# Where weights and features start within 512 bytes: a lead, a slot size and a gap in a float32r decoder trunk

## The chip, the core and the metric

The kernel runs on one core of a Trainium2 chip. The core has TensorE (PE in the profile; its weight loads are shown apart as PEld), VectorE (DVE), ScalarE (ACT), GpSimd (POOL) and SyncE (SP), which here issues nearly all transfers. They share SBUF, 128 partitions of on-chip memory, and TensorE writes its sums to PSUM. A matmul has a stationary operand, which is loaded into the array by a weight load, and a moving operand, which is streamed past it. The metric is the device time of one execution in microseconds (us), as the median of several runs.

## The reference, cut to what matters

Two decoder layers on 256 tokens of width 1024, in float32. Each layer adds four blocks to the residual x:

```python
for l in range(DEPTH):                       # 2 layers
    x = x + 0.5 * swiglu(rms_norm(x, ffn1_norm[l]), gate1[l], up1[l], down1[l])     # 1024 -> 2816 -> 1024
    x = x + hybrid_mixer(rms_norm(x, mix_norm[l]), w_in[l], ..., w_out[l])          # 4 scan heads, 8 softmax heads
    x = x + memory_cross_attention(rms_norm(x, cross_norm[l]), rms_norm(mem, mem_norm[l]),
                                   wq[l], wk[l], wv[l], wo[l])                      # 256 memory tokens
    x = x + 0.5 * swiglu(rms_norm(x, ffn2_norm[l]), gate2[l], up2[l], down2[l])
return rms_norm(x, final_norm)

def swiglu(h, w_gate, w_up, w_down):
    return (silu(h @ w_gate) * (h @ w_up)) @ w_down
```

Nearly all of the work is products of 256 token rows with weight matrices.

## The kernel before

**Precision by splitting.** A float32 product is made of three float32r matmuls. An operand `a` is split into `hi`, its value cast to float32r, and `lo = a - hi`. `mm3` (L441 to L444) then sums `hi*hi`, `hi*lo` and `lo*hi` in PSUM, so each product shows up as one matmul of L442, one of L443 and one of L444. Features are split once per block (`put_split`, L368); weights are split as they come in.

**The plan of weights.** `plan` lists all weight pieces in the order in which they are used: `add_cols` (L90) lists the pieces of a range of columns, four row tiles of 128 each; `add_rows` (L94) those of whole rows of 1024 columns, two row tiles each; `add_ffn` (L98) calls both. `fetch` (L129) loads a piece from HBM into one of three `raw` buffers, by a transfer on SP. `split` (L173) casts it on ScalarE into a `whi` slot and subtracts on VectorE into a `wlo` slot (`split_k`, L145 to L155; L149 and L150 without a gain, L153 and L154 with one). There are seven slots of each kind (`N_W`), of SLOT = 1040 columns. A slot takes two row tiles of 512 columns, one of 1024, or four of 260. `take` (L194) hands out the next piece and has the piece after it split (`LA_S` = 1); the loads run three pieces ahead (`LA_D`). The first two pieces are split block by block in `split_block` (L157).

**Two ways round.** In `wstat` (L566) the weights are stationary and the features move: 256 columns, all tokens, move past a block of 128x128 weights, and the result has features on the partitions. This serves the gate and up projections from the second chunk of columns on, the mixer's gates, queries and keys, and the queries and keys of the cross attention. In `xstat`, `xstat_first`, `first_chunk` and `rows_to_residual` (L450, L460, L482, L637) a block of features is stationary and the weights move, 512 columns at a time (256 or 260 for some): the first chunk of each gate and up projection, the values, the down projections and the output projections. In `rows_to_residual`, while it walks over the row tiles, a slot of one row tile serves twelve matmuls before the next one.

**Memory.** Each pool's tiles lie one behind another in SBUF, in the order of the pools: constants (`cp`), `raw`, the `whi` slots and then the `wlo` slots (`wp`), 19 buffers of 4096 bytes with the tag `s4` (`sp`), which hold the features and nearly all intermediate tiles, then `np` and `sm` with smaller ones, among them `pp` and `ppT`, tiles of the softmax. Below them lie 16384 bytes of scratch for transfer descriptors. Sizes here are bytes per partition.

**Order.** `drive` (L403) runs the main generator and spawned tasks by modelled times, so that small tasks (norms, transposes, softmax heads) are put between the large products in TensorE's instruction stream. In the cross attention, `head` (L1113) uses `mm3` too, without weights: `cs` is the score of a query tile `qc` (stationary) with `kc` (moving), and `cpo` the value tile `vch` or `vcl` (stationary) with the transposed probabilities `ppT` (moving). All of them but `ppT` carry the tag `s4`.

Of the kernel before, what the change touches and what calls it, by code (L numbers as in the profile page):

```python
# [8 lines left out]
F32 = mybir.dt.float32  # L9
# [8 lines left out]
P = 128  # L18
DEPTH = 2
S = 256  # L20
D = 1024
# [4 lines left out]
EPS = 1e-6  # L26
NEG = -1.0e30
FCH = [(c, min(512, DFF - c)) for c in range(0, DFF, 512)]
SLOT = 1040
N_S4, N_W = 19, 7  # L30
TAIL = 6
HP = 100
# [8 lines left out]
OFF_Q, OFF_F, OFF_I, OFF_G = 0, 512, 1024, 1536  # L41
OFF_FQ, OFF_FK, OFF_FV = 2048, 2560, 3072
# [3 lines left out]
def hymba_kernel(  # L46
# [6 lines left out]
    nc = tc.nc  # L53

    cp = ctx.enter_context(tc.tile_pool(name="cp", bufs=1))
    rawp = ctx.enter_context(tc.tile_pool(name="rawp", bufs=3))
    wp = ctx.enter_context(tc.tile_pool(name="wp", bufs=N_W))
    sp = ctx.enter_context(tc.tile_pool(name="sp", bufs=N_S4))
# [7 lines left out]
    def nm(s):  # L66
        uid[0] += 1
        return f"{s}_{uid[0]}"
# [10 lines left out]
    def smp(name="smp"):  # L79
        return pss.tile([P, 512], F32, name=nm(name), tag="smp")  # L80

    xs = cp.tile([P, NT, D], F32, name="xs")


    plan = []

    def kview(w, l, c0, cw, k0, nk):
        return w[l, k0 * P:(k0 + nk) * P, c0:c0 + cw].rearrange("(k p) c -> p k c", p=P)

    def add_cols(w, l, c0, cw, scaled=None):  # L90
        for k0 in range(0, KT, 4):
            plan.append((kview(w, l, c0, cw, k0, 4), 4, cw, (scaled[0], scaled[1] + k0) if scaled else None))

    def add_rows(w, l, nkt):  # L94
        for k0 in range(0, nkt, 2):
            plan.append((kview(w, l, 0, D, k0, 2), 2, D, None))

    def add_ffn(g, u, d, l, scaled=None):  # L98
        for c0, cw in FCH:
            add_cols(g, l, c0, cw, scaled)  # L100
            add_cols(u, l, c0, cw, scaled)
        add_rows(d, l, FT)

    for l in range(DEPTH):
        add_ffn(ffn1_g, ffn1_u, ffn1_d, l, ("first", 0) if l == 0 else None)
        for o in (OFF_I, OFF_G, OFF_F, OFF_Q):
            add_cols(w_in, l, o, 512)
        add_cols(w_in, l, OFF_FV + 260, 260)
        add_cols(w_in, l, OFF_FQ, 512)
        add_cols(w_in, l, OFF_FK, 512)  # L110
        add_cols(w_in, l, OFF_FV, 260)
        of_mem = ("mem", 8 * l)
        add_cols(c_wk, l, 0, 512, of_mem)
        add_cols(c_wk, l, 512, 512, of_mem)
        add_cols(c_wv, l, 0, 512, of_mem)
        add_rows(w_out, l, KT)
        add_cols(c_wv, l, 512, 512, of_mem)
        for c0 in (0, 512):
            add_cols(c_wq, l, c0, 512)
        add_rows(c_wo, l, KT)  # L120
        add_ffn(ffn2_g, ffn2_u, ffn2_d, l)

    raws = []
# [4 lines left out]

    def fetch(i):  # L129
        while len(raws) <= min(i, len(plan) - 1):  # L130
            src, nk, cw, _ = plan[len(raws)]
            r = rawp.tile([P, 4 * 520], F32, name=nm("raw"), tag="raw")
            rv = r[:, :nk * cw].rearrange("p (k c) -> p k c", k=nk)
            n = 4 if len(raws) < 2 else 1
            for k0 in range(0, nk, nk // n):
                nc.sync.dma_start(out=rv[:, k0:k0 + nk // n, :], in_=src[:, k0:k0 + nk // n, :])
                for t, j in ({0: [(1, 0)], 3: [(0, 1), (1, 1)]}.get(k0, []) if not raws else []):
                    load_x(t, j)
            raws.append(r)

    def load_x(t, j):
        sl = slice(j * 512, (j + 1) * 512)
        nc.sync.dma_start(out=xs[:, t, sl], in_=x_d[0, t * P:(t + 1) * P, sl])

    def split_k(i, sl, k, hi, lo):  # L145

        gk = plan[i][3]
        if gk is None:
            nc.scalar.copy(out=hi, in_=sl)  # L149
            nc.vector.tensor_tensor(out=lo, in0=sl, in1=hi.bitcast(F32), op=ALU.subtract)  # L150
        else:
            g = gcols[gk[0]][:, gk[1] + k:gk[1] + k + 1]
            nc.scalar.mul(hi, sl, g)  # L153
            nc.vector.scalar_tensor_tensor(out=lo, in0=sl, scalar=g, in1=hi.bitcast(F32), op0=ALU.mult,  # L154
                                           op1=ALU.subtract)  # L155

    def split_block(i, k):  # L157

        if k == 0:
            fetch(i + LA_D - 1)  # L160
            pieces.append([])
        cw = plan[i][2]
        if k % 2 == 0:
            slot[:] = [wp.tile([P, SLOT], F32R, name=nm(n), tag=n) for n in ("whi", "wlo")]
        sl = slice(k % 2 * cw, (k % 2 + 1) * cw)
        hi, lo = slot[0][:, sl], slot[1][:, sl]
        split_k(i, raws[i][:, k * cw:(k + 1) * cw], k, hi, lo)
        pieces[i].append((hi, lo))
        return [(hi, lo)]
# [3 lines left out]
    def split(i):  # L173
        while len(pieces) <= min(i, len(plan) - 1):
            j = len(pieces)
            fetch(j + LA_D - 1)
            _, nk, cw, gk = plan[j]
            r = raws[j]
            n = max(1, SLOT // cw)
            res = []  # L180
            for k0 in range(0, nk, n):
                kk = min(n, nk - k0)
                sl = r[:, k0 * cw:(k0 + kk) * cw]
                hi = wp.tile([P, SLOT], F32R, name=nm("whi"), tag="whi")
                lo = wp.tile([P, SLOT], F32R, name=nm("wlo"), tag="wlo")
                n1 = kk if gk is None else 1
                for k in range(0, kk, n1):
                    w = slice(k * cw, (k + n1) * cw)
                    split_k(j, sl[:, w], k0 + k, hi[:, w], lo[:, w])
                for k in range(kk):  # L190
                    res.append((hi[:, k * cw:(k + 1) * cw], lo[:, k * cw:(k + 1) * cw]))
            pieces.append(res)

    def take():  # L194
        i = taken[0]
        taken[0] += 1
        split(i + LA_S)
        return pieces[i]
# [18 lines left out]
    for i in range(2):  # L217
        fetch(i)
# [998 lines left out]
```

## Time and profile before

| | |
|---|---|
| median of 3 runs | 1233.07 us (1232.48 to 1235.84) |
| the profiled execution | 1233.42 us |
| its span, first to last instruction | 1231.3 us |
| mean granted TensorE clock | 0.999 |
| read from HBM, mean rate | 216.23 MB, 176 GB/s |

The profile shows one execution. Its page gives, in parts, the engines' busy time, the span in 40 slices, the DMA queues, the chain of work that ended last, the costliest groups of instructions, and the DMA issues. A group's row has the line of the code, engine, operation, what it writes and reads (`out<-in`; for a matmul the moving operand stands first and the stationary one second), shapes, the count, busy time, the mean duration of one, and the idle time just before. Matmuls overlap: one of 256 columns is shown as about 280 ns long, yet the next starts well before it has ended. The timeline has one row per instruction with its start and its duration in us; from two starts and the number of matmuls between them comes the step from one matmul to the next. Addresses aren't in the profile; they follow from the sizes in the code.

### The profile page before, as it was taken

What the parts mean: (1) busy time and instruction counts of PE and PEld (TensorE: products, weight loads), DVE (VectorE), ACT (ScalarE), POOL (GpSimd) and SP (SyncE); (2) the same over time, 40 slices, a digit from 0 to 9 for tenths busy, and PEclk for the clock granted to TensorE, in tenths of its full rate; (3) what the DMA queues carried; (4) which work ended last, traced back from release to release, by engine and by line L of the source; (5) the groups of instructions that cost most, each with busy time, mean ns of one, the idle gap of its engine ahead of it and who ended that gap; (6) DMA issues with size and microseconds to landing.
All of it is one profiled execution on the core that took longest, in us unless ns stands there. A gap on an engine that the chain in (4) does not pass through costs nothing.

```text
span 1231.3 us, 21555 instructions
## 1 busy us (share of the span) xinstructions
PE 1221.1 (99%) x9037; PEld 1117.8 (91%) x9037; DVE 769.6 (63%) x1186; ACT 650.4 (53%) x1014; POOL 37.1 (3%) x50
## 2 busy tenths in 40 slices
PE   9999999999999999999999999999999999999997
PEld 7999888999889889998889998889998898999986
DVE  6966647588866665554474464476787766545643
ACT  7655535578854454444354354266686555443532
POOL 0000000011000000000000000000110000000000
PEclk9999999999999999999999999999999999999999
DMA  8655655642544375565374565465444533555650
GB/s 296 203 177 175 240 196 159 218 159 104 204 141 152 115 244 172 172 223 189 134 256 139 204 201 209 137 222 168 144 138 171 189 137 122 196 179 171 240 171 35
DMA packets 100001, 218.67 MB, mean 178 GB/s; under 512 B 4128, under 2 KB 16704, under 8 KB 99904
## 3 DMA queue, kind: packets, MB, share of 16 engines
q1 hardware_dynamic: 99744, 217.03, 51.8%
q8 instruction: 71, 1.16, 0.4%
q10 hardware_dynamic: 160, 0.27, 0.1%
q14 instruction: 26, 0.21, 0.1%
HBM read 216.23 MB, written 1.05 MB: 176 GB/s over the span
## 4 chain that ended last, share of the span: by engine, by line
PE 93%; DVE 4%; issue 1%; ACT 1%; POOL 1%; DMA 0%; POOLq 0%; ACTq 0%
PE acc L442 28%; PE acc L443 28%; PE acc L444 28%; DVE wlo L150 1%; PE acc L505 1%; PE al L771 1%; DVE wlo L154 1%; PE pt L363 1%; POOL rs L344 1%; PE fs L933 0%; PE fpt L951 0%; DVE xfl L370 0%; PE cpo L443 0%; PE cs L444 0%; PE cs L442 0%
## 5 line engine op out<-in xcount | busy, mean ns | idle before, releaser
L150 DVE TENSOR_TENSOR wlo<-raw,whi 128x1024 fp32r<-128x1024 f32 (+1 forms) x324 | 388.9, 1223 | 265.5 <-ACT whi L149 264.6
L149 ACT CAST whi<-raw 128x1024 fp32r<-128x1024 f32 (+1 forms) x324 | 330.2, 1048 | 276.1 <-PE acc L444 132.5
L442 PE MATMUL acc<-xfh,whi 128*128 128x256 f32 x1536 | 432.2, 282 | 0.0
L443 PE MATMUL acc<-xfl,whi 128*128 128x256 f32 x1536 | 430.7, 280 | 0.3 <-DVE xfl L370 0.2
L444 PE MATMUL acc<-xfh,wlo 128*128 128x256 f32 x1536 | 429.9, 280 | 0.0
L443 PEld LDWEIGHTS acc<-xfl,whi 128*128 128x128 f32 x1536 | 289.3, 188 | 0.9 <-DVE xfl L370 0.7
L444 PEld LDWEIGHTS acc<-xfh,wlo 128*128 128x128 f32 x1536 | 289.3, 188 | 0.0
L442 PEld LDWEIGHTS acc<-xfh,whi 128*128 128x128 f32 x1536 | 288.5, 188 | 0.8
L443 PE MATMUL acc<-wlo,hth 128*128 128x512 f32 (+1 forms) x352 | 136.2, 387 | 0.0
L442 PE MATMUL acc<-whi,hth 128*128 128x512 f32 (+1 forms) x352 | 136.0, 386 | 0.0
L444 PE MATMUL acc<-whi,htl 128*128 128x512 f32 (+1 forms) x352 | 135.6, 385 | 0.0
L442 PE MATMUL acc<-whi,xfh 128*128 128x512 f32 (+1 forms) x240 | 88.0, 367 | 0.0
L443 PE MATMUL acc<-wlo,xfh 128*128 128x512 f32 (+1 forms) x240 | 87.4, 364 | 0.0
L444 PE MATMUL acc<-whi,xfl 128*128 128x512 f32 (+1 forms) x240 | 87.2, 363 | 0.0
L444 PEld LDWEIGHTS acc<-whi,htl 128*128 128x128 f32 x352 | 66.2, 188 | 14.2
L442 PEld LDWEIGHTS acc<-whi,hth 128*128 128x128 f32 x352 | 66.1, 188 | 14.1
L443 PEld LDWEIGHTS acc<-wlo,hth 128*128 128x128 f32 x352 | 66.1, 188 | 13.8
L154 DVE SCALAR_TENSOR_TENSOR wlo<-raw,g,whi 128x512 fp32r<-128x512 f32 (+1 forms) x96 | 62.0, 703 | 18.6 <-PE acc L444 14.9
L153 ACT ACTIVATE whi<-raw,g 128x512 fp32r<-128x512 f32 (+1 forms) x96 | 58.3, 677 | 17.2 <-PE acc L443 14.8
L369 ACT CAST hth<-sil 128x512 fp32r<-128x512 f32 x36 | 22.3, 619 | 57.4 <-DVE sil L738 57.4
L444 PEld LDWEIGHTS acc<-whi,xfl 128*128 128x128 f32 x240 | 45.2, 188 | 7.6
L442 PEld LDWEIGHTS acc<-whi,xfh 128*128 128x128 f32 x240 | 45.1, 188 | 7.7
(274 smaller groups left out, 1547.6 us busy)
## 6 DMA issues: line engine op xcount, KB each, us to landing
raw<-in_ffn_w_down_dram SPq DMA_DIRECT2D x44, 1024.0 KB, 4.9
raw<-in_ffn_w_up_dram SPq DMA_DIRECT2D x40, 1024.0 KB, 5.3
raw<-in_ffn_w_gate_dram SPq DMA_DIRECT2D x38, 1024.0 KB, 5.2
raw<-in_w_in_dram SPq DMA_DIRECT2D x24, 1024.0 KB, 5.3
raw<-in_cross_wk_dram SPq DMA_DIRECT2D x8, 1024.0 KB, 5.4
raw<-in_cross_wv_dram SPq DMA_DIRECT2D x8, 1024.0 KB, 5.2
raw<-in_w_out_dram SPq DMA_DIRECT2D x8, 1024.0 KB, 4.8
raw<-in_cross_wq_dram SPq DMA_DIRECT2D x8, 1024.0 KB, 5.2
```

The lines of the kernel that those rows point to most:

```text
L149: nc.scalar.copy(out=hi, in_=sl)
L150: nc.vector.tensor_tensor(out=lo, in0=sl, in1=hi.bitcast(F32), op=ALU.subtract)
L153: nc.scalar.mul(hi, sl, g)
L154: nc.vector.scalar_tensor_tensor(out=lo, in0=sl, scalar=g, in1=hi.bitcast(F32), op0=ALU.mult, op1=ALU.subtract)
L344: nc.gpsimd.tensor_tensor(out=rs, in0=ms, in1=neghalf[:, 0:1], op=ALU.pow)
L363: nc.tensor.transpose(pt[:, j * P:(j + 1) * P], hn[:, kt * P:(kt + 1) * P], ident)
L369: nc.scalar.copy(out=hi, in_=src)
L442: nc.tensor.matmul(ps, lhsT=lh, rhs=rh, start=start, stop=False)
L443: nc.tensor.matmul(ps, lhsT=lh, rhs=rl, start=False, stop=False)
L444: nc.tensor.matmul(ps, lhsT=ll, rhs=rh, start=False, stop=stop)
L505: nc.tensor.matmul(psa_[t], lhsT=x, rhs=w, start=kt == 0 and which == 0, stop=kt == KT - 1 and which == 1)
L771: nc.tensor.matmul(ps[s0:s0 + hb, c0:c0 + hb], lhsT=k[:, h, a:a + hb], rhs=rhs[:, h, a + step:a + step + hb], start=True, stop=True)
```

## The change

The slots become 1152 columns (4608 bytes), a multiple of 512 bytes. Row tiles within a slot start at multiples of 512 columns (256 for pieces of 256 columns), so that a 260-column row tile takes the room of 512 and a slot holds two of them. Each plan entry carries a lead: stationary weights start 16 columns (64 bytes) into their slot, moving ones at its start. A tile of 64 columns (256 bytes), `apart`, is put ahead of the `s4` buffers. To make room, the `raw` buffers lose 32 columns each and the scratch for transfer descriptors is halved to 8192 bytes. The products, their order and the loads stay.

```diff
-SLOT = 1040
+ROWS, LEAD = 1024, 16
+SLOT = ROWS + 128
+APART = 64
...
+    sp.tile([P, APART], F32, name="apart", tag="apart", bufs=1)
     xs = cp.tile([P, NT, D], F32, name="xs")
...
-    def add_cols(w, l, c0, cw, scaled=None):
+    def add_cols(w, l, c0, cw, scaled=None, lead=LEAD):
         for k0 in range(0, KT, 4):
-            plan.append((kview(w, l, c0, cw, k0, 4), 4, cw, (scaled[0], scaled[1] + k0) if scaled else None))
+            plan.append((kview(w, l, c0, cw, k0, 4), 4, cw, (scaled[0], scaled[1] + k0) if scaled else None, lead))
...
-            plan.append((kview(w, l, 0, D, k0, 2), 2, D, None))
+            plan.append((kview(w, l, 0, D, k0, 2), 2, D, None, 0))
...
-            add_cols(g, l, c0, cw, scaled)
-            add_cols(u, l, c0, cw, scaled)
+            for w in (g, u):
+                add_cols(w, l, c0, cw, scaled, LEAD if c0 else 0)
...
-            add_cols(w_in, l, o, 512)
-        add_cols(w_in, l, OFF_FV + 260, 260)
+            add_cols(w_in, l, o, 512, None, 0 if o in (OFF_I, OFF_G) else LEAD)
+        add_cols(w_in, l, OFF_FV + 260, 260, None, 0)
...
-            r = rawp.tile([P, 4 * 520], F32, name=nm("raw"), tag="raw")
+            r = rawp.tile([P, 4 * 512], F32, name=nm("raw"), tag="raw")
...
-            n = max(1, SLOT // cw)
+            step = 256 if cw == 256 else max(512, cw)
+            n = ROWS // step
...
+                hv, lv, rv = (a[:, b:b + kk * st].rearrange("p (k c) -> p k c", k=kk)[:, :, 0:cw]
+                              for a, b, st in ((hi, lead, step), (lo, lead, step), (sl, 0, cw)))
                 n1 = kk if gk is None else 1
                 for k in range(0, kk, n1):
-                    w = slice(k * cw, (k + n1) * cw)
-                    split_k(j, sl[:, w], k0 + k, hi[:, w], lo[:, w])
+                    w = slice(k, k + n1)
+                    split_k(j, rv[:, w], k0 + k, hv[:, w], lv[:, w])
                 for k in range(kk):
-                    res.append((hi[:, k * cw:(k + 1) * cw], lo[:, k * cw:(k + 1) * cw]))
+                    res.append((hv[:, k], lv[:, k]))
...
-    nc = _bacc.Bacc("TRN2", target_bir_lowering=False, num_devices=1)
+    nc = _bacc.Bacc("TRN2", target_bir_lowering=False, num_devices=1, dynamic_dma_scratch_size=8192)
```

The other 260-column piece and the values of the cross attention (`c_wv`) get a lead of 0 in the same way.

More of the change, by code (lines that the diff above doesn't have):

```diff
@@ L106, in hymba_kernel @@
         for o in (OFF_I, OFF_G, OFF_F, OFF_Q):
-            add_cols(w_in, l, o, 512)
-        add_cols(w_in, l, OFF_FV + 260, 260)
+            add_cols(w_in, l, o, 512, None, 0 if o in (OFF_I, OFF_G) else LEAD)
+        add_cols(w_in, l, OFF_FV + 260, 260, None, 0)
         add_cols(w_in, l, OFF_FQ, 512)
         add_cols(w_in, l, OFF_FK, 512)
-        add_cols(w_in, l, OFF_FV, 260)
+        add_cols(w_in, l, OFF_FV, 260, None, 0)
         of_mem = ("mem", 8 * l)
@@ L114, in hymba_kernel @@
         add_cols(c_wk, l, 512, 512, of_mem)
-        add_cols(c_wv, l, 0, 512, of_mem)
+        add_cols(c_wv, l, 0, 512, of_mem, 0)
         add_rows(w_out, l, KT)
-        add_cols(c_wv, l, 512, 512, of_mem)
+        add_cols(c_wv, l, 512, 512, of_mem, 0)
         for c0 in (0, 512):
@@ L130, in fetch @@
         while len(raws) <= min(i, len(plan) - 1):
-            src, nk, cw, _ = plan[len(raws)]
-            r = rawp.tile([P, 4 * 520], F32, name=nm("raw"), tag="raw")
+            src, nk, cw, _, _ = plan[len(raws)]
+            r = rawp.tile([P, 4 * 512], F32, name=nm("raw"), tag="raw")
             rv = r[:, :nk * cw].rearrange("p (k c) -> p k c", k=nk)
@@ L176, in split @@
             fetch(j + LA_D - 1)
-            _, nk, cw, gk = plan[j]
+            _, nk, cw, gk, lead = plan[j]
             r = raws[j]
-            n = max(1, SLOT // cw)
+            step = 256 if cw == 256 else max(512, cw)
+            n = ROWS // step
             res = []
```

## The prediction

> **What bounds the kernel now.** I read the page from the top: the engines' busy time, the granted clock, the chain that ended last, then the groups.
>
> ```profile
> span 1231.3 us, 21555 instructions
> ## 1 busy us (share of the span) xinstructions
> PE 1221.1 (99%) x9037; PEld 1117.8 (91%) x9037; DVE 769.6 (63%) x1186; ACT 650.4 (53%) x1014; POOL 37.1 (3%) x50
> ...
> PEclk9999999999999999999999999999999999999999
> ...
> PE 93%; DVE 4%; issue 1%; ACT 1%; POOL 1%; DMA 0%; POOLq 0%; ACTq 0%
> ...
> L150 DVE TENSOR_TENSOR wlo<-raw,whi 128x1024 fp32r<-128x1024 f32 (+1 forms) x324 | 388.9, 1223 | 265.5 <-ACT whi L149 264.6
> L149 ACT CAST whi<-raw 128x1024 fp32r<-128x1024 f32 (+1 forms) x324 | 330.2, 1048 | 276.1 <-PE acc L444 132.5
> ```
>
> The matmuls are the bound: PE is busy for 99% of the span at the full clock and makes 93% of the chain. The weight splits (cast on ACT, subtraction on DVE) wait for PE to give slots back, not the reverse. So the time is the number of matmuls times the step from one to the next. The mean of one (282 ns) is no step, as matmuls overlap; I take the step from the timeline, first start to last start of an unbroken stretch, and the count from the groups in the same stretch. Weights stationary (256 moving columns), in FFN 2 of the first layer:
>
> ```profile
> L442 PE MATMUL acc<-xfh,whi 128*128 128x256 f32 x279 | 78.2, 280 | 0.0
> L443 PE MATMUL acc<-xfl,whi 128*128 128x256 f32 x279 | 78.2, 280 | 0.0
> L444 PE MATMUL acc<-xfh,wlo 128*128 128x256 f32 x279 | 78.1, 280 | 0.0
> ```
> ```profile
> 457.02 0.36 PE L442 MATMUL acc<-xfh,whi 128*128 128x256 f32 x1
> ...
> 555.41 0.27 PE L444 MATMUL acc<-xfh,wlo 128*128 128x256 f32 x1
> ```
>
> 3·279 = 837 matmuls start in 98.39 us: 98.39/836 = **117.7 ns** a step. Weights moving (512 columns), the down projection of FFN 1:
>
> ```profile
> L442 PE MATMUL acc<-whi,hth 128*128 128x512 f32 x85 | 33.4, 392 | 0.0
> ```
> ```profile
> 135.14 0.39 PE L442 MATMUL acc<-whi,hth 128*128 128x512 f32 x1
> ...
> 193.84 0.39 PE L444 MATMUL acc<-whi,htl 128*128 128x512 f32 x1
> ```
>
> 3·85 = 255 matmuls in 58.70 us: 58.70/254 = **231.1 ns**. Nothing interrupts either stretch, so whatever varies in these steps is TensorE's own. The numbers of such matmuls in the kernel, by form:
>
> ```profile
> L442 PE MATMUL acc<-xfh,whi 128*128 128x256 f32 x1536 | 432.2, 282 | 0.0
> ...
> L442 PE MATMUL acc<-whi,hth 128*128 128x512 f32 x330 | 129.9, 394 | 0.0
> ...
> L442 PE MATMUL acc<-whi,xfh 128*128 128x512 f32 x176 | 69.6, 396 | 0.0
> ...
> L442 PE MATMUL acc<-mfh,whi 128*128 128x256 f32 x128 | 36.9, 288 | 0.0
> ...
> L442 PE MATMUL acc<-whi,mfh 128*128 128x512 f32 x64 | 25.8, 403 | 0.0
> L442 PE MATMUL acc<-whi,oTh 128*128 128x512 f32 x64 | 25.3, 396 | 0.0
> L442 PE MATMUL acc<-whi,cTh 128*128 128x512 f32 x64 | 25.2, 399 | 0.0
> ...
> L505 PE MATMUL acc<-whi,xfh 128*128 128x512 f32 x16 | 7.0, 449 | 0.3 <-ACT xfh L369 0.2
> ```
>
> Every matmul of L442 comes three times (L442, L443, L444): (1536+128)·3 = **4992** with stationary weights, about 587 us, and (330+176+64+64+64)·3 + 48 of L505 = **2142** with moving ones, about 495 us. These two are the span but for 150 us.
>
> **Does the step depend on addresses?** Call distance the start of the stationary operand less that of the moving one, modulo 512 bytes. By the sizes in the code and the allocation of the program before, whi slots start at 55232 + 4160k, wlo at 84352 + 4160k, features (tag s4) at 113472 + 4096k and ppT at 219648 + 2048k. So features lie at 320 modulo 512, ppT at 0, and since 4160 = 8·512 + 64 the seven slots of each half lie 64 bytes apart, and wlo 64 before its whi. The distance of a weight changes every 6 to 12 matmuls, and 117.7 and 231.1 are means over seven distances. The cross attention holds it still, in the same L442 to L444 and the same 128x256 form: cs has two features (distance 0), cpo has vch or vcl stationary (320) over ppT (0), distance 320.
>
> ```profile
> 380.31 0.28 PE L442 MATMUL cs<-kc,qc 128*128 128x256 f32 x1
> ...
> 381.63 0.28 PE L444 MATMUL cs<-kc,qc 128*128 128x256 f32 x1
> ```
> ```profile
> 409.06 0.28 PE L442 MATMUL cpo<-ppT,vch 128*128 128x256 f32 x1
> ...
> 410.31 0.28 PE L444 MATMUL cpo<-ppT,vcl 128*128 128x256 f32 x1
> 410.42 0.39 PE L442 MATMUL acc<-whi,cTh 128*128 128x512 f32 x1
> ```
> ```profile
> 1000.77 0.28 PE L442 MATMUL cpo<-ppT,vch 128*128 128x256 f32 x1
> ...
> 1002.06 0.28 PE L444 MATMUL cpo<-ppT,vcl 128*128 128x256 f32 x1
> ```
>
> Twelve matmuls each. cs at distance 0: 1.32/11 = **120.0 ns**. cpo at distance 320: (410.42−409.06)/12 = **113.3 ns**, although ACT was casting weights at that time, and in the run at 1000.77 1.29/11 = 117.3. So a constant distance settles TensorE into a fixed rhythm that depends on the distance; 320 has a fast rhythm, into which it need not fall at once.
>
> [...]
>
> **The change part by part.** Scratch 16384 to 8192 bytes, raw 3·8320 to 3·8192: whi begins at 55232 − 8192 − 384 = 46656, which is 64 modulo 512. Slots of 1152·4 = 4608 = 9·512 keep all fourteen at 64. The 256 bytes of `apart` put the features at 46656 + 14·4608 + 256 = 111424, again 320. Hence stationary weights (lead 64) lie at 128: distance 128 − 320, that is **320, always**, the distance of cpo. Moving weights lie at 64: distance **256, always**. What lies behind the features moves by 2048 = 4·512 with them, so cs and cpo keep their distances.
>
> *Stationary weights.* The nearest rows are cpo's: 113.3 settled, 117.3 in a run that did not settle within 12. In stretches as long as 837 I give the unsettled rhythm a fifth: 0.8·113.3 + 0.2·117.3 = 114.1. Gain 4992·(117.7 − 114.1) ns = **18.0 us**. Ends: 113.3 throughout gives 22.0; 117.3 gives 2.0; a rhythm like that of cs, 120.0, costs 11.5.
>
> *Moving weights.* No row has both halves at 256. In the down projection each slot serves 12 matmuls before the next; these are a slot with whi at 256 (wlo at 320), one of the fastest, and one of the usual slow ones:
>
> ```profile
> 580.49 0.39 PE L442 MATMUL acc<-whi,hth 128*128 128x512 f32 x1
> ...
> 583.25 0.39 PE L442 MATMUL acc<-whi,hth 128*128 128x512 f32 x1
> ```
> ```profile
> 338.40 0.39 PE L442 MATMUL acc<-whi,oTh 128*128 128x512 f32 x1
> ...
> 341.14 0.40 PE L442 MATMUL acc<-whi,oTh 128*128 128x512 f32 x1
> ```
> ```profile
> 137.90 0.40 PE L442 MATMUL acc<-whi,hth 128*128 128x512 f32 x1
> ...
> 140.68 0.40 PE L442 MATMUL acc<-whi,hth 128*128 128x512 f32 x1
> ```
>
> 2.76, 2.74 and 2.78 us for twelve: 230.0, 228.3 and 231.7 ns. I take the first, its distance being nearest: gain 2142·(231.1 − 230.0) ns = **2.4 us**. A settled rhythm can lie outside mixed ones, as cpo lies 4.4 below the mixed 117.7 and cs 2.3 above: 226.7 would gain 9.4 us, 233.4 would cost 4.9.
>
> *What it adds.* A 260-column load (8 in all) used one slot of 1040 columns and now uses two of 2·260, so 8 more casts and 8 more subtractions. By L149 and L150 one on all 1024 columns takes 1.05 and 1.22 us; eight more of half that size are at most 4.2 and 4.9 us in all, beside PE work on engines busy for 53 and 63%; without that cover they would cost up to those. They also take 8 more of the slots that PE gives back; with seven slots and one load split ahead, two loads hold at most four. Casts into 512-column strides and the 64-byte lead leave the elements the same; I take 0, as both engines wait for PE (276.1 and 265.5 us idle), and bound it by a tenth of L150's time, 39 us spread over a lane with 265 us idle: still covered. The matmuls with 260 columns go from a mixed distance to 256; I leave them at 0.
>
> *DMA and scratch.* The same loads of the same bytes go out on SP, in order; raw buffers only start elsewhere:
>
> ```profile
> raw<-in_ffn_w_down_dram SPq DMA_DIRECT2D x44, 1024.0 KB, 4.9
> raw<-in_ffn_w_up_dram SPq DMA_DIRECT2D x40, 1024.0 KB, 5.3
> ```
>
> Each lands in about 5 us, while PE needs some 5.6 us for the two slots of a load (48 matmuls), with three buffers in the ring. No row shows a load issued by POOL, so I cost the smaller scratch at 0; were it to slow loads, the ring covers some 5 us of lateness per load.
>
> *Sum.* No wait is added on PE. A step gained is gained in the span, as PE is never out of work in these stretches; ACT and DVE, at 53 and 63%, would rise to 54 and 64%, so they aren't next. 18.0 + 2.4 = 20.4 us. The profiled execution took 1233.42 us, 2.1 us around its span of 1231.3; its time is 0.35 above the median of 1233.07. So 1233.1 − 20.4 = 1212.7, **1213 us**.
>
> **Rivals.**
> 1. *Nothing settles*: operands are read independently, or interruptions and mixed addresses of other engines keep the slow rhythm. For: the cpo run at 1000.77, 117.3 over all 12. Against: 409.06, settled from its first matmul under load. Gain 0 to 2.0 us: 1231 to 1233. [...]
> 2. *A slow rhythm locks in* (slower): a constant distance holds a bad rhythm as firmly as a good one, as cs does at 120.0. At 120.0 stationary (+11.5) and 231.7 moving (+1.3) it is 1246 us. With moving ones unchanged it decides from a stationary step of 118.4 on (0.3% of the time over 4992 steps above 117.7). For: the cs run never leaves 120. Against: cs is at 0; stationary weights come to 320, where 120 was not held.
> 3. *Both lock fast*: 113.3 (−22.0) and 226.7 (−9.4): 1202 us. For: both constants hold over whole stages. Against: no run of twelve with moving weights lies under 228.
>
> **Chances.** Forecast 0.62; nothing settles 0.15 (two thirds of it the independent reads); slow rhythm 0.08; both fast 0.15. Measurement can tell about 0.3%, or 3.7 us. Faster holds the forecast, the third rival and a trifle of the first: 0.78; same 0.14; slower 0.08. The range reaches over both fast (1202, and 2 us for a still faster moving step) and nothing settles: 1200 to 1233; it leaves out the slow rhythm (0.08) and some 0.05 below. The forecast alone spans 1206 to 1222.
>
> **What would show it.** In the stretch of 837 the step should be 113 to 115 ns, 3.6 ns less; in that of 255 about 230. cs must stay at 120.0 and cpo at 113 to 118, since their distances stay. PE stays at 99%, its matmul counts unchanged, L149 and L150 eight or more instances up with the same mean. I am wrong on the mechanism if the step of 837 stays at 117.7, or if cs or cpo moves along with it; wrong on the cover if PE shows new idle time after L149 or L150; wrong on a size if the step of 255 leaves 228 to 232.

## The result and the profile after

The changed kernel takes 1218.48 us (median of 4 runs, 1216.27 to 1220.5) against 1232.91 for the kernel before: a ratio of 0.9881, with a 95% interval of 0.9862 to 0.9900. Its four times are not spread evenly: 1216.27, 1216.61, 1220.35 and 1220.5.

The page of the profiled execution (1216.61 us), in the same parts as before; L449 to L451 are now the three matmuls of `mm3`, L153 and L154 cast and subtraction:

```profile
span 1214.8 us, 21577 instructions
...
PE 1201.1 (99%) x9037; PEld 1104.8 (91%) x9037; DVE 769.8 (63%) x1194; ACT 651.5 (54%) x1022; POOL 37.7 (3%) x50
...
PE 87%; DVE 5%; ACT 4%; issue 2%; POOL 1%; DMA 1%; POOLq 0%; SPq 0%; ACTq 0%
...
L154 DVE TENSOR_TENSOR wlo<-raw,whi 128x1024 fp32r<-128x1024 f32 (+1 forms) x332 | 389.6, 1196 | 255.3 <-ACT whi L153 253.0
L153 ACT CAST whi<-raw 128x1024 fp32r<-128x1024 f32 (+1 forms) x332 | 331.9, 1029 | 263.9 <-PE acc L451 126.7
```

The same 9037 matmuls, at the same granted clock (0.999), take 20.0 us less of PE's time, while the span is 16.5 us shorter: PE is idle for some 3.5 us more, and PE's share of the chain falls from 93 to 87%. There are 8 more casts and subtractions.

The timeline shows where the time went. Two stretches of 837 matmuls with stationary weights, first and last start of each (each has 279 of L449, L450 and L451), and one of 255 matmuls with moving weights:

```profile
452.13 0.36 PE L449 MATMUL acc<-xfh,whi 128*128 128x256 f32 x1
...
550.68 0.28 PE L451 MATMUL acc<-xfh,wlo 128*128 128x256 f32 x1
...
638.19 0.37 PE L449 MATMUL acc<-xfh,whi 128*128 128x256 f32 x1
...
733.04 0.28 PE L451 MATMUL acc<-xfh,wlo 128*128 128x256 f32 x1
```
```profile
130.81 0.40 PE L449 MATMUL acc<-whi,hth 128*128 128x512 f32 x1
...
188.41 0.39 PE L451 MATMUL acc<-whi,htl 128*128 128x512 f32 x1
```

98.55/836 = **117.9 ns**, 94.85/836 = **113.5 ns** and 57.60/254 = **226.8 ns**. The same kind of work, with the same distances, runs in two rhythms, called the long and the short one below: one long stretch gained nothing, the other 4.2 ns a step. Moving weights gained 4.3 ns a step. The list of PE's waits has rows that it did not have:

```profile
PE acc L451 <- DVE wlo L154: 0.9, 2, 0.5
...
PE acc L451 <- DVE wlo L158: 0.5, 1, 0.5
```

They are the price of the changed slots (see the run with 260 columns packed): PE waits for a subtraction. Other waits have grown too, among them that of L450 for `xfl`, 0.8 us where it was 0.2; that one stays when the columns are packed, so it has another cause, which is open.

### The profile page after: what moved, and what is told of

Its sections match the earlier page's. It is cut to its first block, busy times and chain, and to the rows that moved or that the text cites. A ratio compares the mean times of both kernels' runs of the same rounds, so it can differ in the third digit from the quotient of the medians.

```text
span 1214.8 us, 21577 instructions
## 1 busy us (share of the span) xinstructions
PE 1201.1 (99%) x9037; PEld 1104.8 (91%) x9037; DVE 769.8 (63%) x1194; ACT 651.5 (54%) x1022; POOL 37.7 (3%) x50
## 4 chain that ended last, share of the span: by engine, by line
PE 87%; DVE 5%; ACT 4%; issue 2%; POOL 1%; DMA 1%; POOLq 0%; SPq 0%; ACTq 0%
PE acc L449 27%; PE acc L451 27%; PE acc L450 27%; DVE wlo L154 1%; ACT whi L157 1%; DVE wlo L158 1%; PE acc L512 1%; DMA mem<-in_mem_dram 1%; PE pt L370 1%; POOL rs L351 1%; PE al L778 0%; ACT whi L153 0%; DVE xfl L377 0%; ACT pp L902 0%; POOL hrs L847 0%
## 5 line engine op out<-in xcount | busy, mean ns | idle before, releaser
L154 DVE TENSOR_TENSOR wlo<-raw,whi 128x1024 fp32r<-128x1024 f32 (+1 forms) x332 | 389.6, 1196 | 255.3 <-ACT whi L153 253.0
L153 ACT CAST whi<-raw 128x1024 fp32r<-128x1024 f32 (+1 forms) x332 | 331.9, 1029 | 263.9 <-PE acc L451 126.7
L449 PE MATMUL acc<-xfh,whi 128*128 128x256 f32 x1536 | 428.8, 279 | 0.0
L451 PE MATMUL acc<-xfh,wlo 128*128 128x256 f32 x1536 | 427.1, 278 | 0.9 <-DVE wlo L154 0.9
L450 PE MATMUL acc<-xfl,whi 128*128 128x256 f32 x1536 | 427.1, 278 | 0.8 <-DVE xfl L377 0.8
L449 PEld LDWEIGHTS acc<-xfh,whi 128*128 128x128 f32 x1536 | 290.0, 189 | 0.8
L450 PEld LDWEIGHTS acc<-xfl,whi 128*128 128x128 f32 x1536 | 289.2, 188 | 1.4 <-DVE xfl L377 1.3
L451 PEld LDWEIGHTS acc<-xfh,wlo 128*128 128x128 f32 x1536 | 288.4, 188 | 1.3 <-DVE wlo L154 1.3
L449 PE MATMUL acc<-whi,hth 128*128 128x512 f32 (+1 forms) x352 | 135.0, 384 | 0.0
L450 PE MATMUL acc<-wlo,hth 128*128 128x512 f32 (+1 forms) x352 | 134.8, 383 | 0.0
L451 PE MATMUL acc<-whi,htl 128*128 128x512 f32 (+1 forms) x352 | 134.6, 383 | 0.0
L449 PE MATMUL acc<-whi,xfh 128*128 128x512 f32 (+1 forms) x240 | 87.3, 364 | 0.0
L451 PE MATMUL acc<-whi,xfl 128*128 128x512 f32 (+1 forms) x240 | 86.6, 361 | 0.0
L450 PE MATMUL acc<-wlo,xfh 128*128 128x512 f32 (+1 forms) x240 | 86.5, 360 | 0.0
L451 PEld LDWEIGHTS acc<-whi,htl 128*128 128x128 f32 x352 | 66.1, 188 | 13.0
L449 PEld LDWEIGHTS acc<-whi,hth 128*128 128x128 f32 x352 | 66.2, 188 | 12.9
L450 PEld LDWEIGHTS acc<-wlo,hth 128*128 128x128 f32 x352 | 66.2, 188 | 12.8
L451 PEld LDWEIGHTS acc<-whi,xfl 128*128 128x128 f32 x240 | 45.1, 188 | 6.9
L449 PEld LDWEIGHTS acc<-whi,xfh 128*128 128x128 f32 x240 | 45.1, 188 | 6.9
```

What stands on the lines that cost most here:

```text
L449: nc.tensor.matmul(ps, lhsT=lh, rhs=rh, start=start, stop=False)
L450: nc.tensor.matmul(ps, lhsT=lh, rhs=rl, start=False, stop=False)
L451: nc.tensor.matmul(ps, lhsT=ll, rhs=rh, start=False, stop=stop)
```

## The experiments

Steps in the tables are worked out like those above, from the first and the last start of a stretch and the number of steps between; the stretches are those of the four FFNs (723 matmuls in the first, 837 in the others) and of their down projections (255, and 54 in the last). A single time stands for one execution; beside it the kernel before took 1234.15 us in the first four runs and 1232.42 in the next three. Other executions of the kernel before took 1232.27 to 1235.84. From here on distances are given modulo 256; the first runs show why.

**The changed kernel once more.** No edit.

> The changed kernel as it is, once more. Theory A (two rhythms at distance 320; which one a stretch falls into is decided by the moment at which it begins, not by the program): each long stretch with stationary weights runs at either 113.4 or 117.8 ns a step, but the slow one need not be that at 452 us again; the time is near 1216.5 with one long stretch in the slow rhythm, 1220.3 with two, 1212.8 with none (837 x 4.4 ns = 3.7 us each). Rival B (the slow stretch is set by the program: its slots, its place in the order): the stretch that begins near 452 us is slow again and the other three are fast, and times differ for another reason.

1216.48 us. The stretches are at 113.5, 113.5, 117.9 and 113.5 ns:

```profile
451.95 0.37 PE L449 MATMUL acc<-xfh,whi 128*128 128x256 f32 x1
...
546.80 0.28 PE L451 MATMUL acc<-xfh,wlo 128*128 128x256 f32 x1
...
634.37 0.36 PE L449 MATMUL acc<-xfh,whi 128*128 128x256 f32 x1
...
732.91 0.28 PE L451 MATMUL acc<-xfh,wlo 128*128 128x256 f32 x1
```

The long rhythm has moved from the stretch at 452 to that at 634 us with not one instruction changed, so it isn't set by the program (rival B falls). The first steps of the stretches, in ns from start to start, tell which one it becomes:

```
run, stretch   first steps                          then
after, 452     201 117 118 118 118 117 119 117      117.9
after, 638     202 121 116 114 114 113 113 114      113.5
again, 452     201 122 116 114 113 114 113 113      113.5
again, 634     201 118 117 119 117 118 118 117      117.9
```

The rhythm is there by the fourth step and then holds for more than 800.

**Without the lead**

```diff
-ROWS, LEAD = 1024, 16
+ROWS, LEAD = 1024, 0
```

> Stationary weights without their lead, so at 64 modulo 512 with the features at 320: distance 256 instead of 320; moving weights stay at 256. Theory A (the distance alone sets the step): the stretches with stationary weights leave 113.4; a slot with distance 256 showed 118 in the kernel before, so 117 to 120 ns and 1220 to 1233 us. Rival C (slots that are a multiple of 512 bytes are enough, the lead does nothing): 113.4 and 117.8 as in the changed kernel, 1213 to 1220 us. Stretches with moving weights stay at 226.8 under both.

1238.71 us: above every time of the kernel before. All long stretches are at 120.1 ns, in one rhythm:

```profile
458.81 0.36 PE L449 MATMUL acc<-xfh,whi 128*128 128x256 f32 x1
...
559.21 0.28 PE L451 MATMUL acc<-xfh,wlo 128*128 128x256 f32 x1
```

100.40/836. Moving weights stay at 226.8. So 64 bytes of lead are worth 2.2 to 6.6 ns of every such step, by the rhythm, and aligned slots alone (rival C) are worse than the mixed distances of before. At distance 256 the step is the 120 that the scores of the cross attention (cs) have at distance 0.

**A lead for each FFN, two runs**

```diff
+    LEADS = [(4, 0), (5, 1), (6, 2), (7, 3)]
...
+        st, mv = LEADS.pop(0)
...
-                add_cols(w, l, c0, cw, scaled, LEAD if c0 else 0)
-        add_rows(d, l, FT)
+                add_cols(w, l, c0, cw, scaled, 16 * st if c0 else 0)
+        add_rows(d, l, FT, 16 * mv)
```

The second run has the pairs (0, 4), (1, 5), (2, 6), (3, 7).

> Another lead in each of the four FFNs, all else as in the changed kernel: distances of stationary weights 0, 64, 128, 192 in the order of time (long stretches near 50, 455, 640, 1060 us), of moving weights 256, 192, 128, 64 (near 133, 550, 735, 1190 us). Theory A: each stretch has a step of its own; 0 gives 120.0 as the scores of the cross attention do; the others hold a constant value between 113.3 and 122; moving at 256 gives 226.8, the others up to 7 ns more or less. Rival C: all at 113.4 or 117.8 and 226.8.

> As the run before, with distances of stationary weights 256, 320, 384, 448 in the order of time and of moving weights 0, 448, 384, 320. Theory A: stationary at 320 gives 113.4 or 117.8, the first (256) what the run without the lead shows; moving at 320 below or at 226.8, at 0 above it. Rival C: all at 113.4 or 117.8 and 226.8.

1229.54 and 1228.33 us. In the first of them the four long stretches, at distances 0, 64, 128 and 192:

```profile
49.64 0.39 PE L451 MATMUL acc<-xfh,whi 128*128 128x256 f32 x1
...
136.37 0.28 PE L453 MATMUL acc<-xfh,wlo 128*128 128x256 f32 x1
...
458.24 0.37 PE L451 MATMUL acc<-xfh,whi 128*128 128x256 f32 x1
...
553.09 0.28 PE L453 MATMUL acc<-xfh,wlo 128*128 128x256 f32 x1
...
641.27 0.37 PE L451 MATMUL acc<-xfh,whi 128*128 128x256 f32 x1
...
740.56 0.28 PE L453 MATMUL acc<-xfh,wlo 128*128 128x256 f32 x1
...
1061.18 0.36 PE L451 MATMUL acc<-xfh,whi 128*128 128x256 f32 x1
...
1159.72 0.28 PE L453 MATMUL acc<-xfh,wlo 128*128 128x256 f32 x1
```

```
distance in bytes           0 / 256   64 / 320   128 / 384   192 / 448
stationary, first run ns    120.1     113.5      118.8       117.9
stationary, second run      120.1     113.5      118.8       117.9
moving, first run           226.8     233.3      232.4       228.9
moving, second run          226.8     233.3      232.4       228.9
```

All distances of the second run are 256 bytes from those of the first, and the steps agree to 0.1 ns. So at these distances the step goes by 256 bytes, not by 512. The table also shows that both offsets of the change are the best of the four, 64 for stationary weights (in the long rhythm level with 192) and 0 for moving ones. Exchanged, they are the worst.

**The same distance without a lead**

```diff
-ROWS, LEAD = 1024, 16
-APART = 64
+ROWS, LEAD = 1024, 0
+APART = 48
```

> No lead, and the gap ahead of the features 192 bytes instead of 256: weights at 64, features at 256 modulo 512, so stationary weights at distance -192, which is 64 modulo 256, and moving weights at 192. Theory A (the distance modulo 256 alone sets the step): stationary stretches at 113.4 or 117.8 ns as in the changed kernel although no weight has a lead, moving ones at 228.9 as in the run with distance 192. Rival D (the place of an operand itself, weights 64 bytes off or features at 320, sets it): stationary ones at 120.1 as without the lead, moving ones at 226.8. The scores of the cross attention keep 120.0 under A.

1227.53 us. The moving step is 228.9, as the table has it for 192:

```profile
133.49 0.39 PE L449 MATMUL acc<-whi,hth 128*128 128x512 f32 x1
...
191.63 0.40 PE L451 MATMUL acc<-whi,htl 128*128 128x512 f32 x1
...
455.52 0.36 PE L449 MATMUL acc<-xfh,whi 128*128 128x256 f32 x1
...
554.06 0.28 PE L451 MATMUL acc<-xfh,wlo 128*128 128x256 f32 x1
```

The long stretches with stationary weights are at 113.5, 117.9, 117.9 and 117.9, and the two of 192 behind moving weights, at 117.8 in the changed kernel, at 113.5. Both rhythms of distance 64 are there, and nowhere the 120.1 that the same weight slots have with the features at 320. So it is the distance that counts, not the place of either operand (rival D falls).

**An unneeded transpose at an entry**

```diff
+        kick = smp("kick")
+        nc.tensor.transpose(kick[:, 0:P], ident, ident)
         yield from wstat(f, gates)
```

> The changed kernel with one unneeded transpose (128 columns, into a spare PSUM tile) ahead of the gates of the mixer, where 192 matmuls with stationary weights follow matmuls with moving ones directly and ran at 117.78 ns in both profiles of the changed kernel. Theory A (the moment of entry picks one of two rhythms at distance 64, and it is then held): with another entry at least one of the two stretches near 214 and 817 us starts with steps like 201, 122, 116 and holds 113.4, 0.8 us less for each, against some 0.2 us for the transpose. Rival E (the slow rhythm belongs to the place: this stage's features, slots or neighbours): both stay at 117.8.

1221.38 us. Both stretches change over: their steps begin with 202, 117, 117, 123, 118 and settle at 113.3, with a mean of 113.9:

```profile
217.38 0.36 PE L449 MATMUL acc<-xfh,whi 128*128 128x256 f32 x1
...
239.14 0.28 PE L451 MATMUL acc<-xfh,wlo 128*128 128x256 f32 x1
```

21.76 us for 191 steps against 22.50 in the changed kernel: the gain of the 0.8 us expected less what the entry costs. The stretch is the same work at the same place, so its rhythm is that of its entry (rival E falls). The time as a whole is no verdict here: two of the long stretches were in the long rhythm, and the first long stretch began at 51.34 us, 2.6 us later than in the changed kernel, ahead of anything that the edit touches. From there to the end it took 1168.3 us against 1166.1; one more stretch in the long rhythm costs 3.7 and the two new entries give 1.5, which is that difference.

**Finer distances**, with leads of 8, 12, 20 and 24 columns for stationary and 4, 8, 60 and 56 for moving weights.

> Finer distances, in bytes modulo 256: stationary 32, 48, 80, 96 in the order of time (long stretches near 50, 455, 640, 1060 us), moving 240, 224, 16, 32 (near 133, 550, 735, 1190 us). Theory A with a step that changes in whole pieces of 64 bytes: each distance behaves like a multiple of 64 next to it (stationary 113.4, 117.8, 118.8 or 120.1; moving 226.8, 228.9 or 232.4). Theory A': finer distances have rhythms of their own, between or outside these; a stationary one that has 113.4 alone, or a moving one under 226.8, would beat the changed kernel. Rival C (the lead does nothing) has fallen already.

1235.64 us. Stationary at 32, 48, 80 and 96 bytes: 118.5, 117.9, 118.8 and 118.8 ns. Moving at 240, 224, 16 and 32: 231.6, 233.3, 236.6 and 233.2. The slowest of them:

```profile
744.83 0.39 PE L451 MATMUL acc<-whi,hth 128*128 128x512 f32 x1
...
804.92 0.40 PE L453 MATMUL acc<-whi,htl 128*128 128x512 f32 x1
```

60.09/254. Steps of their own lie between multiples of 64 (theory A with whole pieces of 64 bytes falls), for moving weights up to 9.8 ns above that at 0. None of the eight beats the two in the change.

**The changed kernel, timed again**

> The changed kernel, timed five times more. Theory A: its executions fall on levels some 3.7 us apart (837 x 4.4 ns) by the number of long stretches with the slow rhythm: near 1212.8, 1216.5, 1220.3, 1224; the profiled one lies on the level that its stretches give. Rival B' (noise from elsewhere): times spread evenly between 1216 and 1221, or the profile's slow stretches don't go with its time.

1219.76, 1220.08, 1220.55 and 1221.32 us. The profiled one, 1220.55, has two long stretches in the long rhythm, at 452 and at 1053 us; the two profiles before it, 1216.61 and 1216.48, have one. Three profiles lie on the levels that their stretches give, 837·4.4 ns = 3.7 us apart. No execution at 1212.8 was seen.

**Four row tiles of 260 columns in one slot again**

```diff
-            step = 256 if cw == 256 else max(512, cw)
-            n = ROWS // step
+            step = cw if cw in (256, 260) else max(512, cw)
+            n = 4 * 260 // step
```

> Only the 260-column pieces go back to four row tiles in one slot (1040 columns, row tiles 1040 bytes apart, so their distance is no longer constant). Theory F (the new idle time of PE before L451 near 246, 247 and 883 us comes from the two slots that such a piece takes now): these waits, 0.4, 0.5 and 0.5 us in the list of waits, go, and 1 to 2 us of the time with them, while the 192 matmuls of 260 columns go from 118.7 to some 119.8 ns, 0.2 us. Rival G (the splits are late there because PE itself is faster): the waits stay. Long stretches may be in either rhythm, worth 3.7 us each, so the waits decide, not the time.

1214.57 us with one long stretch in the long rhythm, where the changed kernel has 1216.5. All that the list of waits has for PE from 0.6 us up:

```profile
PE warm L234 <- POOL ident masks.py:199: 1.4, 1, 1.4
PE fs L940 <- DVE AX L849: 1.1, 1, 1.1
PE acc L450 <- DVE xfl L377: 0.8, 2, 0.4
PE fpt L958 <- DVE oTl L377: 0.6, 1, 0.6
```

The waits of L451 for a split are gone, and the step of the 260-column matmuls goes from 118.7 to 119.2 ns. Counted from the start of the first long stretch, which came 0.8 us later here (49.53 against 48.74), the gain is 3.2 us, 2.3 of them before the second long stretch begins. Dividing a piece over two slots was the cause (theory F). The run takes back two things at once, the second slot and the extra cast and subtraction. For the slot speaks that in the changed kernel ACT stood idle ahead of a cast for such a piece until PE had done a matmul:

```profile
235.31 0.63 ACT L153 CAST whi<-raw 128x520 fp32r<-128x520 f32 x1 [2.82 <-PE acc L450]
```

Rival G holds in part: without the lead, where PE is slower, the two rows of waits are 0.5 and 0.2 us instead of 0.9 and 0.5.

**Transposes at five entries, alone and with the packing.** The edit: the transpose ahead of the mixer's gates, and in the three later FFNs between gate and up projection, so that 768 of the 837 matmuls of a long stretch come behind it

```diff
+                if ci == 1 and not first:
+                    kick()
                 yield from wstat(f, use_u, cw)
```

> An unneeded transpose ahead of the mixer's gates, as in the run before, and one between gate and up projection of the second chunk in the three FFNs whose long stretch follows eight transposes. Theory A: a single transpose after running matmuls led into the fast rhythm every time so far, so whatever follows it holds 113.4 in all long stretches; times lie on one level, near 1213 (1212.8 less twice 0.6 us, plus five transposes of 0.2 us), 0.4% under the changed kernel. Rival: the entry stays a matter of chance, with levels 3.7 us apart as before, 1212 to 1222.

> Both: the transposes of the run before and four row tiles of 260 columns in one slot. Theory A and F: 1 to 2 us under the run with the transposes alone, near 1211.5. Rival: no difference to it.

1223.63 us (1223.03 to 1224.15, five runs; ratio to the kernel before 0.9921, 0.9907 to 0.9934) and 1221.40 us (0.9905, 0.9891 to 0.9918). My guess of the direction was wrong: behind this transpose all three long stretches went into the long rhythm, in both profiles, six of six, three of them with the short rhythm ahead and three with the long one:

```profile
460.82 0.27 PE L574 MATMUL kick<-ident 128*128 128x128 f32 x1
460.85 0.36 PE L449 MATMUL acc<-xfh,whi 128*128 128x256 f32 x1
...
551.26 0.28 PE L451 MATMUL acc<-xfh,wlo 128*128 128x256 f32 x1
```

90.41 us for 767 steps, 117.9. But the first run's times now keep to one level (1.1 us from lowest to highest, where the changed kernel's nine span 5.1), as one expects when every execution enters in the same way. The second lies 2.2 us lower, as the packing had given. In it one of the two stretches at the gates did not change over, so that entry is not sure either.

**A smaller transpose**

```diff
+        nc.tensor.transpose(smp("kick")[:, 0:24], lbr, ident[0:24, 0:24])
```

in place of the full one in the FFNs, none at the gates, with the packing.

> Four row tiles of 260 columns in one slot, and between gate and up projection of the second chunk in the three later FFNs the small transpose (24 columns) of L310 once more, in place of the full one that led into the slow rhythm six times of six. The stretch of the first FFN, which begins behind that small transpose, was in the fast rhythm (113.5) in every profile with distance 64, with the steps 222, 117, 117, 123, 118, 113. Theory A (the entry picks the rhythm, which is then held): the three long stretches behind it hold 113.4 in every execution, one level of times near 1212 (1214.6 with one slow stretch, less 3.7, plus three times 0.3 us). Rival H (the entry depends on more than the kind of matmul ahead, such as the rhythm before it): some of the three are at 117.9, as a whole or by chance, and times lie between 1212 and 1222.

1216.70 us (1214.90 to 1219.24; ratio 0.9857, 0.9837 to 0.9876). In the profiled execution (1219.24) one stretch went into the short rhythm and two into the long one, and what stood ahead explains which:

```profile
459.03 0.24 PE L574 MATMUL kick<-ident,lbr 24*128 24x24 f32 x1
459.20 0.39 PE L449 MATMUL acc<-xfh,whi 128*128 128x256 f32 x1
...
546.25 0.28 PE L451 MATMUL acc<-xfh,wlo 128*128 128x256 f32 x1
...
641.78 0.24 PE L574 MATMUL kick<-ident,lbr 24*128 24x24 f32 x1
641.95 0.38 PE L449 MATMUL acc<-xfh,whi 128*128 128x256 f32 x1
...
732.39 0.28 PE L451 MATMUL acc<-xfh,wlo 128*128 128x256 f32 x1
```

```
transpose at   steps ahead of it        steps behind it                  then
49.16 (L317)   118 118 117 118 118      223 117 117 123 118 112 115      113.5
459.03         118 117 119 117 118      223 116 118 122 119 113 113      113.5
641.78         113 114 113 113 114      221 118 117 119 117 118 118      117.9
1058.86        114 113 114 113 113      222 117 118 118 117 118 118      117.9
```

87.05 and 90.44 us for 767 steps. It exchanged the rhythms: long became short and short became long, four of four here. The transpose at L317, which every version has ahead of its first long stretch, turned long into short in all nine profiles with distance 64 there. Rival H has it: behind this transpose, the entry depends on the rhythm ahead. Behind the transpose of 128 columns in the FFNs it did not.

In the changed kernel eight transposes (L700) stand ahead of each stretch of 837. There the choice shows before them, in the step from the last matmul to the first transpose. Two entries of the changed kernel, at 452 and 638 us:

```profile
451.22 0.28 PE L451 MATMUL acc<-xfh,wlo 128*128 128x256 f32 x1
451.35 1.03 PE L700 MATMUL hp<-ident,sil 128*128 128x128 f32 x8
...
637.28 0.28 PE L451 MATMUL acc<-xfh,wlo 128*128 128x256 f32 x1
637.40 1.04 PE L700 MATMUL hp<-ident,sil 128*128 128x128 f32 x8
```

In ns these steps are 122 and 118. In the five profiles with this entry and the long rhythm ahead (the three of the changed kernel, the first transpose run and the packing), 122 or 123 led into the long rhythm seven times of seven, 117 or 118 into the short one eight times of eight. So the choice seems to be made at the end of the stretch ahead, not by the transposes. What sets that step is open. With the short rhythm ahead, in the run with the gap of 192 bytes, the same eight transposes were followed by the long one three times of three.

The 1216.70 us are the lowest time of all versions that were timed more than once. That the transposes add to it is not shown: the packing alone was at 1214.57 in its one execution. The interval lies below that of the changed kernel's second timing (0.9883 to 0.9910) and overlaps that of its first.

## Why the prediction was right, and where its sizes were off

The forecast of 1213 us, with 1200 to 1233, met 1218.5; the gain of 20.4 us came out as 14.4, and as 16.5 between the two profiled spans. That the total came this near is in part luck: one term was 9 us too large, the other some 5 too small.

**The mechanism held.** PE stayed the bound, busy for 99% of the span before and after. A constant distance gives a rhythm, and that of distance 320, read from twelve matmuls of cpo, is that of the weights: 113.5 where 113.3 was read, and 117.9 where the run at 1000.77 had 117.3. With the moving operand in its place, 64 bytes of lead of the stationary one made 120.1 into 113.5 or 117.9 (the run without the lead against the change).

The prediction counted distances modulo 512 bytes where the steps repeat every 256; nothing in its sum hangs on that.

The step goes with where the two operands lie to each other: 113.5 to 120.1 ns for 256 moving columns at distances of 0, 64, 128 and 192 bytes. No run shows what in TensorE makes it so.

**The term for stationary weights was too large.** The step that failed is "in stretches as long as 837 I give the unsettled rhythm a fifth". I took 117.3 for a beginning that settles; it is a second rhythm, as stable as the first. In the profiled execution the four long stretches gave 10.0 us (98.39, 98.40, 98.37 and 85.01 us became 98.55, 94.85, 94.85 and 81.95), and all of this form, from each of the 4992 to the matmul behind it, waits included, 9.0 (593.2 us became 584.2) of the 18.0 forecast. The short stretches gave nothing in sum: those of 192, behind moving weights, entered the long rhythm both times. Some three fifths of these steps are of the short rhythm in that execution (2957 of 4992 last 115 ns or less) and two fifths in the one with two long stretches in the long rhythm (2108), not four fifths. Of the stretches of 837, four of nine were in the long rhythm in the three profiles, where the prediction had a fifth.

**The term for moving weights was too small.** I took 230.0 from a slot whose two halves lay at 256 and 320. At 256 alone the step is 226.8, outside the 228 to 232 that it gave for a right size. The prediction had 226.7 as the end of its range, got by moving cpo's lead over the mixed mean. That this came true is luck: it carried a difference of 256 moving columns at 64 over to 512 at 0, and the table shows that the two forms do not follow each other. Summed over the 2062 steps between neighbouring matmuls of 512 columns that are not interrupted (300 ns or less), it is 468.9 us against 476.5, 7.6 us instead of 2.4.

**The cover failed in part.** Eight more casts and subtractions were costed at nothing because their engines wait for PE. The engines do (263.9 us of idle time ahead of L153, 126.7 of it until a matmul of L451, and 255.3 ahead of L154, 253.0 of it until L153), but the pieces behind the 260-column ones came late: waits of 0.9 and 0.5 us, gone with the packing, and with them 2.0 us between single executions with the same number of long rhythms. The prediction counted how busy the engines are on average; what it left out is when a split comes in its place, behind a slot that PE must first give back. The slot's part in that is argued from the 2.82 us of idle time above, not shown by a run of its own. The halved scratch and the raw buffers cost nothing that a profile shows: a load into a raw buffer lands in 5.2 us before and 5.1 after (medians), and PE waits for none of them. Neither was tried alone.

**The rivals.** "A slow rhythm locks in" was a real danger with another place: without the lead it is what happens, at 120.1 and 1238.7 us. "Nothing settles" came near the step of the long rhythm, 117.9, but not to its nature: that rhythm is settled. That operands are read independently, two thirds of that rival's chance, no run shows; the runs show a step that goes with the distance, 113.5 to 120.1 ns. "Both lock fast" was right for moving weights alone. The sign that I gave of a wrong mechanism, cs leaving 120.0, did not come: its uninterrupted steps are 119.7 ns on average before and 119.8 after, and those of cpo 115.0 and 116.0, within the 113 to 118 that were forecast.

What stays open: why there are two rhythms at distance 64, and what exactly an entry must do to lead into the short one. In these runs the rhythm ahead, the last step ahead and the kind of matmul at the entry go with the choice; no edit was found that leads into the short rhythm every time.

## What to carry to other kernels

When a stretch of matmuls runs unbroken at the full clock (0.999 granted here), its step from start to start is worth a look by operand addresses: here the distance of stationary and moving operand modulo 256 bytes made 113.5 to 120.1 ns for 256 columns, and a slot pitch that is no multiple of 256 mixes several of them (117.7 ns as the mean over seven slots, 4160 bytes apart). A dozen matmuls elsewhere in the same trace that happen to hold the distance constant foretold the step before anything was built. They also showed two rhythms, 113.3 and 117.3 ns, and the second was taken for a start that settles: read from them whether there are one or two. Where times fall on levels, count in each profile which stretches are on which side before a difference of that size is called an effect.

## What the runs showed of the hardware that I had not expected

The step repeats with the distance by 256 bytes, to 0.1 ns: 120.1, 113.5 or 117.9, 118.8 and 117.9 ns at 0, 64, 128 and 192 for 256 moving columns, and 226.8, 233.3, 232.4 and 228.9 for 512, where the best place for one form is the worst for the other. At distance 64 TensorE has two stable rhythms, 113.5 and 117.9 ns, taken up within some six steps of an entry and held for more than 800 matmuls, while ACT and DVE work beside it (busy for 54 and 63% of the changed kernel's span). A transpose of 24 columns ahead of a stretch changed one rhythm into the other, in either direction. Where eight transposes stand ahead, the rhythm could be told from the last step before them: 122 or 123 ns ahead of the long one, 117 or 118 ahead of the short one, fifteen times of fifteen with the long rhythm ahead.
